# Final norm ahead of the overflow branch, a router norm for each half of the rows, and gated products on VectorE: a single-core diffusion block

## The chip, the cores and the metric

The kernel runs on one core of one Trainium2 chip. A core has the matmul engine TensorE (PE, its weight loads are listed apart as PEld), VectorE (DVE), ScalarE (ACT), GpSimd (POOL) and SyncE (SP), and DMA engines that move data between HBM and the on-chip memories. The metric is the device time of one execution in microseconds (us). The time before is the median of three runs; the trace is one more execution under the hardware profiler.

## What is computed

One layer of a diffusion backbone on 256 latent rows of 1024 features, with 256 rows of context. Cut to what matters here:

```
h      = modulate(rms_norm(x, g_mix))             # also for the context
u,v,yg,xr,ga,gb = split(h @ w_in + b_in)
a_lat  = layer_norm(conv31(u * sigmoid(v)));  a_lat = silu(a_lat) @ w_pa
y_rec  = rglru forward + rglru backward           # linear scans along the rows
b_lat  = (gelu(yg) * y_rec) @ w_pb                # the gated products
x      = x + gt1 * ((sigmoid(ga) * a_lat + sigmoid(gb) * b_lat) @ w_o)
hm     = modulate(rms_norm(x, g_ffn))             # the router's norm
gates  = top-1 of 4 groups, top-2 of 4 experts in it, from hm @ w_grp, hm @ w_er
x      = x + gt2 * sum over experts of swiglu(hm; w_gate, w_up, w_down) * gates
return   rms_norm(x, g_final)                     # the final norm
```

All is float32. A large matmul is made of float32r pieces: each operand is split into a high part (a ScalarE copy to float32r) and a low part (a subtraction), and three products are added.

## The kernel before

`hybrid_block` holds the whole layer. Rows lie in two blocks of 128 (index b), features in two halves of 512 (index h) or eight tiles of 128 (index t). Weights of `w_in`, `w_pb`, `w_pa` and `w_o` arrive as `raw` tiles; ScalarE (L291) and VectorE (L292) split each into `ws`, and `project` (matmuls on L307) uses them. Expert weights `ew` stream in through SyncE's and GpSimd's queues as their buffers come free. What stands on each engine comes from a scheduler, which may move instructions; those given to `pin` (`tc.keep_in_program_order`), `fix` and `in_order` keep their written order.

Four places matter.

**Gated products.** After the scans, the gate `gT` is multiplied by the scans' sum `yl` in four pieces of 128x512 (`prods`, L796), ScalarE rounds each to `mh` (L800), and the rest goes to `ml` (L801). Both L796 and L801 run on GpSimd. Behind that the layer norm of the convolution branch: squares `t` of `yc` (L816, ScalarE, out of the same pool `tmp` of rotating buffers as the products), their mean by a matmul (L817), `lm` (L819), a root, `yc` times the root (L824), swish, and the split into `ah` (ScalarE) and `al` (L831, GpSimd). `mh`, `ml` feed the `w_pb` projection and `ah`, `al` the `w_pa` projection; L844 merges the first into the sum.

**Root.** `rsqrt` takes a shift and a subtraction on the bits, and three Newton steps. For a width of 2 each step runs column by column (L207, L210), otherwise on the whole (L212 to L214).

**Router.** In the `w_o` loop each block gets its residual (L956, L957), the modulated `xs` (L959), the square sums `ssq2`, a transpose, and logits (`logits`, L935). `stay_warm(n)` issues n matmuls without use (L915) to keep TensorE busy; `WARM` has the four counts. After both blocks the root of both columns is taken at once (`ms2`, L986), the logits are scaled (`lg20`, L990), ranked, and the chosen experts' mask `mskb` (L1070) goes to the counting matmul `utri` (L1074). From the counts come positions and the one-hot rows `sg`, and only then the low parts `xsl` of the second half (`low_part`, L920), which gather matmuls (L1029) read.

**Tail.** Four groups of experts run with fixed capacities. Then a condition (`count(0)`, kept in `cint`) says whether any expert has overflowed; if so, nested blocks of extra work run. With these inputs they do not. Behind the branch (L1381) comes the final norm: `ms3` (L1394) and its root, two products with `gfin` on GpSimd (L1399) that ScalarE scales, two on VectorE (L1403), and the output's transfers, two from SyncE's queue (L1404) and two from ScalarE's (L1406).

## Time and profile before

| what | value |
|---|---|
| median of three runs | 604.14 us (604.13 to 605.14) |
| the profiled execution, its own time | 605.15 us |
| its span in the trace | 603.3 us |
| mean granted TensorE clock | 0.977 |
| busy: PE, PEld, DVE, ACT, POOL | 562.9, 371.7, 332.1, 249.1, 115.5 us |
| bytes moved | 182.86 MB, mean 303 GB/s |

The span is what the trace covers; the execution's own time is 1.85 us longer. Busy times are sums over each engine's instructions; engines run side by side, so they don't add up to the span. Idle time before an instruction is put down to what ended last before it started.

### The profile page before, as it was taken

The numbers are of one execution on the slowest core, as the hardware profiler recorded it, in microseconds if no ns is written. First come the engines' busy times: TensorE is split into PE (matmuls) and PEld (weight loads), VectorE is DVE, ScalarE is ACT, GpSimd is POOL, SyncE is SP. The second block draws the span as 40 slices with busy tenths as digits, with TensorE's granted clock in tenths as the row PEclk, the third lists the DMA queues.
The fourth block names the chain that finished last, engine by engine and source line by source line (L and its number), as shares of the span: only waits on it lengthen the run. The fifth ranks groups of instructions, "written<-read, shape, count | busy, mean of one in ns | idle before, by whom it ended". The sixth has DMA issues, their size and how long they took to land. (4 is left out here: it accounts for less than half of the span.)

```text
span 603.3 us, 9530 instructions
## 1 busy us (share of the span) xinstructions
PE 562.9 (93%) x3864; PEld 371.7 (62%) x3864; DVE 332.1 (55%) x658; ACT 249.1 (41%) x394; POOL 115.5 (19%) x122
## 2 busy tenths in 40 slices
PE   9989899999999999998999999969999999999980
PEld 8778777767667687788999787333335335333420
DVE  4724784821088978998897757623143404523224
ACT  4315524465954999646583552120012002101101
POOL 0000200001000100028072000333333431244301
PEclk9989899999999999999999999998999999999996
DMA  8982897368454467757975966799999999999942
GB/s 342 421 359 82 312 380 265 122 241 346 140 198 148 182 212 279 279 202 284 423 283 210 381 258 266 297 422 420 422 422 421 420 422 421 375 377 422 419 175 73
DMA packets 31326, 182.86 MB, mean 303 GB/s; under 512 B 3710, under 2 KB 8086, under 8 KB 10796
## 3 DMA queue, kind: packets, MB, share of 16 engines
q1 hardware_dynamic: 18812, 98.21, 42.9%
q0 software_dynamic: 12032, 83.35, 33.8%
q8 instruction: 32, 0.52, 0.4%
q10 hardware_dynamic: 432, 0.62, 0.3%
q14 instruction: 18, 0.15, 0.1%
HBM read 179.53 MB, written 2.64 MB: 302 GB/s over the span
## 5 line engine op out<-in xcount | busy, mean ns | idle before, releaser
L292 DVE TENSOR_TENSOR ws<-raw,ws 128x1024 fp32r<-128x1024 f32 x72 | 92.2, 1302 | 66.8 <-ACT ws L291 62.7
L307 PE MATMUL acca<-hxh,ws 128*128 128x256 f32 (+1 forms) x384 | 106.3, 320 | 2.4 <-ACT hxh L258 2.0
L307 PE MATMUL accb<-hxh,ws 128*128 128x256 f32 (+1 forms) x384 | 99.6, 302 | 0.0
L291 ACT ACTIVATE ws<-raw 128x1024 fp32r<-128x1024 f32 x72 | 74.2, 1053 | 26.4 <-PE accb L307 14.9
L307 PEld LDWEIGHTS acca<-hxh,ws 128*128 128x128 f32 x384 | 68.0, 192 | 16.9 <-issue 9.9
L307 PEld LDWEIGHTS accb<-hxh,ws 128*128 128x128 f32 x384 | 68.1, 192 | 2.9 <-ACT th L388 0.4
L1237 PE MATMUL acca<-ew,hg 128*64 128x512 f32 (+1 forms) x320 | 59.2, 595 | 0.0
L307 PE MATMUL acca<-hxl,ws 128*128 128x256 f32 (+1 forms) x192 | 55.2, 305 | 0.1
L307 PE MATMUL accb<-hxl,ws 128*128 128x256 f32 (+1 forms) x192 | 54.8, 303 | 0.0
L1237 PE MATMUL accb<-ew,hg 128*64 128x512 f32 (+1 forms) x256 | 45.1, 594 | 0.0
L307 PEld LDWEIGHTS acca<-hxl,ws 128*128 128x128 f32 x192 | 37.1, 193 | 4.4 <-issue 2.9
L597 POOL DMA_INDIRECT ew<-in_w_gate_dram,idxd x24 | 23.2, 967 | 86.8 <-PE acca L1237 45.9
L1237 PEld LDWEIGHTS acca<-ew,hg 128*64 128x64 f32 (+1 forms) x320 | 17.2, 126 | 35.5 <-issue 34.5
L307 PEld LDWEIGHTS accb<-hxl,ws 128*128 128x128 f32 x192 | 37.2, 194 | 1.3
L1250 PE MATMUL accb<-ew,at 128*32 128x512 f32 (+1 forms) x128 | 25.7, 675 | 6.2 <-DMA ew<-in_w_down_dram 3.9
L1200 ACT ACTIVATE yh<-yv 128x512 fp32r<-128x512 f32 x12 | 7.6, 630 | 56.5 <-DVE yv L1195 56.5
L667 PE MATMUL side<-xc,gw 128*128 128x512 f32 x64 | 30.6, 602 | 0.0
L1212 DVE TENSOR_TENSOR xt<-xt,side 128x512 f32<-128x512 f32 x28 | 18.2, 684 | 21.1 <-PE side L1211 21.0
L597 POOL DMA_INDIRECT ew<-in_w_down_dram,idxd x24 | 22.8, 951 | 36.3 <-issue 12.4
L1250 PE MATMUL acca<-ew,at 128*64 128x512 f32 (+1 forms) x128 | 25.4, 654 | 4.6 <-ACT at L1291 2.6
L1237 PEld LDWEIGHTS accb<-ew,hg 128*64 128x64 f32 (+1 forms) x256 | 12.8, 123 | 27.2 <-issue 27.2
L377 PE MATMUL side<-z,csw 128*32 128x256 f32 x512 | 29.0, 380 | 0.0
(343 smaller groups left out, 986.2 us busy)
## 6 DMA issues: line engine op xcount, KB each, us to landing
raw<-in_w_in_dram SPq DMA_DIRECT2D x24, 1024.0 KB
raw<-in_w_rows_dram SPq DMA_DIRECT2D x16, 1024.0 KB
wsc<-in_w_mod_dram SPq DMA_DIRECT2D x8, 1024.0 KB
ew<-in_w_gate_dram SPq DMA_DIRECT2D x8, 1024.0 KB
ew<-in_w_up_dram SPq DMA_DIRECT2D x8, 1024.0 KB
ew<-in_w_down_dram SPq DMA_DIRECT2D x8, 1024.0 KB
z<-zd POOLq DMA_DIRECT2D x8, 766.0 KB, 7.7
csw<-in_conv_s_dram SPq DMA_DIRECT2D x4, 1024.0 KB
```

What stands on the lines that cost most here:

```text
L291: S.activation(w[:, 0], src, AF.Copy)
L292: io(V.tensor_tensor(w[:, 1], src, w[:, 0].bitcast(F32), op=ALU.subtract))
L307: ins = io(T.matmul(o, l[pr[0]], r[pr[1]], start=start and first.get(i) == j and not (paired and i % 2), stop=stop and j >= len(n) - m and ...
L377: T.matmul(o[32 * i:32 * i + 32], csw[t // 2][:, t % 2, i, m], z[:, i, :, 4 * m:4 * m + 64], start=(m == 0), stop=(m == 7))
L597: return P.indirect_dma_start(out=t.rearrange("p k c -> p (k c)"), out_offset=None, in_=wex[key].rearrange("e (r k) c -> (e r) (k c)", k=m ...
L667: T.matmul(o1, gws[g][:, d, m, t], xcs[g][:, t].rearrange("p s n -> p (s n)"), start=True, stop=True)
L1200: S.activation(yh, yv, AF.Copy)
L1212: V.tensor_tensor(xt[:, b, cs], xt[:, b, cs], po, op=ALU.add)
L1237: fix(T.matmul(o[j][n * i:n * i + n, :], sl(i, k), wt[p, key, i, k // 4][:, k % 4, :], start=(k == 0), stop=(k == 7)))
L1250: fix(T.matmul(od[c][n * i:n * i + n, :], at[:, k, n * i:n * i + n], wt[p, 2, i, h][:, k % 2, 512 * c:512 * c + 512], start=(k == 0), stop ...
```

## The change

In words: (1) the products `prods` and the remainders `ml` of the gated products are issued on VectorE instead of GpSimd. (2) A new function `root(b)` takes the root of one block's `ssq2` alone, right after that block's logits in the second half of the `w_o` loop; `low_part(0, 1)` is pinned right behind `root(0)` and no longer behind the one-hot rows; the scaling into `lg20` is pinned; `rsqrt` runs column by column for a width of 1 too; the third entry of `WARM` goes from 13 to 11. (3) A new function `final_norm()` is called ahead of the branch, and again inside the overflow block at its end (where the rows are written a second time, behind the first writes). In it one 128x512 piece is multiplied by `gfin` on VectorE before the root and scaled by ScalarE, the other three are made by VectorE in one operation each, and all four transfers are issued by SyncE.

```diff
-WARM = (3, 3, 13, 3)
+WARM = (3, 3, 11, 3)
...
         for _ in range(3):
-            if n == 2:
+            if n <= 2:
                 for b in range(n):
...
     for t in range(0, 8, 2):
         prods.append(tmp([128, 2, 256]))
-        P.tensor_tensor(prods[-1], gT[:, t:t + 2], yl[:, t:t + 2], op=ALU.mult)
+        V.tensor_tensor(prods[-1], gT[:, t:t + 2], yl[:, t:t + 2], op=ALU.mult)
...
         S.activation(mh[:, t:t + 2], prods[t // 2], AF.Copy)
-        P.tensor_tensor(ml[:, t:t + 2], prods[t // 2], mh[:, t:t + 2].bitcast(F32), op=ALU.subtract)
+        V.tensor_tensor(ml[:, t:t + 2], prods[t // 2], mh[:, t:t + 2].bitcast(F32), op=ALU.subtract)
...
+    r2s = [None, None]
+
+    def root(b):
+        in_order[0] = V.engine
+        ms2 = cp.tile([128, 1], F32, name=f"ms2{b}")
+        io(V.scalar_tensor_tensor(ms2, ssq2[:, b, 0:1], EPS, ssq2[:, b, 1:2], op0=ALU.add, op1=ALU.add))
+        r2s[b] = rsqrt(ms2, [128, 1], lambda s, n: cp.tile(s, F32, name=f"r2{b}" + n))
+        in_order[0] = T.engine
...
                 logits(b, h, turn(b, h))
+                root(b)
+                if b == 0:
+                    pin(low_part(0, 1))
...
-    ms2 = cp.tile([128, 2], F32, name="ms2")
-    after(V.scalar_tensor_tensor(ms2, ssq2[:, :, 0], EPS, ssq2[:, :, 1], op0=ALU.add, op1=ALU.add), x_ins)
-    r2 = rsqrt(ms2, [128, 2], lambda s, n: cp.tile(s, F32, name="r2" + n))
-    r2s = [r2[:, b:b + 1] for b in range(2)]
     for b in range(2):
-        V.scalar_tensor_tensor(lg20[:, b], plg[b], r2s[b], br20, op0=ALU.mult, op1=ALU.add)
+        pin(V.scalar_tensor_tensor(lg20[:, b], plg[b], r2s[b], br20, op0=ALU.mult, op1=ALU.add))
...
     sg0 = slots_of((pos[:, :, STATIC[0]:STATIC[0] + 4], CAP // 2), first=True)
-    pin(low_part(0, 1))
     pin(low_part(1, 1))
...
+    def final_norm():
+
+        xg = [[tmp([128, 512], name="xg") for _ in range(2)] for _ in range(2)]
+        ms3 = eps[0].tile([128, 2], F32, name="ms3", tag="ms3", bufs=2)
+        V.tensor_tensor(xg[0][0], xt[:, 0, 0:512], gfin[:, 0:512], op=ALU.mult)
+        V.scalar_tensor_tensor(ms3, ssq3[:, :, 0], EPS, ssq3[:, :, 1], op0=ALU.add, op1=ALU.add)
+        r3 = rsqrt(ms3, [128, 2], lambda s, n: eps[0].tile(s, F32, name="r3" + n, tag="r3" + n, bufs=2))
+        S.activation(xg[0][0], xg[0][0], AF.Copy, scale=r3[:, 0:1])
+        for b, h in ((0, 0), (1, 0), (1, 1), (0, 1)):
+            hs = slice(512 * h, 512 * h + 512)
+            if b + h:
+                V.scalar_tensor_tensor(xg[b][h], xt[:, b, hs], r3[:, b:b + 1], gfin[:, hs], op0=ALU.mult, op1=ALU.mult)
+            ins = dma(ov_[:, b, hs], xg[b][h])
...
+    written = {}
+    final_norm()
+
+
     with tc.If(count(0) > 0):
         extra_pair()
...
-    for h in range(2):
-        hs = slice(512 * h, 512 * h + 512)
-        P.tensor_tensor(xg[h], xt[:, 0, hs], gfin[:, hs], op=ALU.mult)
-    r3 = rsqrt(ms3, [128, 2], lambda s, n: cp.tile(s, F32, name="r3" + n))
-    for h in range(2):
-        hs = slice(512 * h, 512 * h + 512)
-        V.scalar_tensor_tensor(xg[2 + h], xt[:, 1, hs], r3[:, 1:2], gfin[:, hs], op0=ALU.mult, op1=ALU.mult)
-        dma(ov_[:, 1, hs], xg[2 + h])
-        S.activation(xg[h], xg[h], AF.Copy, scale=r3[:, 0:1])
-        dma2(ov_[:, 0, hs], xg[h])
+        final_norm()
```

How it moves instructions: VectorE, around the gated products, where `t_...` are the products, L292 the weight splits, L710 to L714 the end of the scans; rows of the kernel before carry a minus, of the changed one a plus.

```order
+L796 TENSOR_TENSOR t_2715<-gT,yl 128x512
+L796 TENSOR_TENSOR t_2717<-gT,yl 128x512
 L712 SCALAR_TENSOR_TENSOR t_2567<-la,t_2567,lt 128x256
 L714 TENSOR_TENSOR yl<-yl,t_2567 128x256
-L292 TENSOR_TENSOR ws<-raw,ws 128x1024 x6
+L292 TENSOR_TENSOR ws<-raw,ws 128x1024 x2
+L801 TENSOR_TENSOR ml<-t_2715,mh 128x512
+L796 TENSOR_TENSOR t_2719<-gT,yl 128x512
+L796 TENSOR_TENSOR t_2721<-gT,yl 128x512
+L292 TENSOR_TENSOR ws<-raw,ws 128x1024
+L801 TENSOR_TENSOR ml<-t_2717,mh 128x512
+L292 TENSOR_TENSOR ws<-raw,ws 128x1024 x2
```

The eight operations of GpSimd now stand between the weight splits on VectorE; two more of `ml` and two splits follow, and then `lm`, with seven splits ahead of it in all where there were six.

Further on, on VectorE too, one split has left the root of the layer norm and the first pair of merges (L844) stands ahead of `yc`.

```order
-L292 TENSOR_TENSOR ws<-raw,ws 128x1024
 L212 TENSOR_TENSOR rst<-rsy 128x256
 L213 TENSOR_TENSOR rst<-rst,rsh 128x256
 L214 SCALAR_TENSOR_TENSOR rsy<-rst,rsy 128x256
-L824 TENSOR_TENSOR yc<-yc,rsy 128x256 x8
 L844 SCALAR_TENSOR_TENSOR tga_2345<-tga_2345,acca 128x512
 L844 SCALAR_TENSOR_TENSOR tga_2345<-tga_2345,accb 128x512
+L824 TENSOR_TENSOR yc<-yc,rsy 128x256 x8
```

One of the two splits inside the root is gone, and the merges, which stood behind `yc`, have moved in front of it.

VectorE in the router before, from the second half's first block on (`t_3601`: block 0, `t_3623`: block 1):

```order
L956 TENSOR_TENSOR t_3601<-acca,rw_3104 128x512
L957 TENSOR_TENSOR xt<-xt,t_3601 128x512
L959 TENSOR_TENSOR xs<-xt,rw_3104 128x512
L956 TENSOR_TENSOR t_3623<-accb,rw_3104 128x512
L957 TENSOR_TENSOR xt<-xt,t_3623 128x512
L959 TENSOR_TENSOR xs<-xt,rw_3104 128x512
L986 SCALAR_TENSOR_TENSOR ms_3666<-ssq_3425 128x2
L199 TENSOR_SCALAR r2rsy<-ms_3666 128x2
```

And the same place after the change, with line numbers of the changed kernel:

```order
L968 TENSOR_TENSOR xs<-xt,rw_3104 128x512
L954 SCALAR_TENSOR_TENSOR ms_3623<-ssq_3425 128x1
L199 TENSOR_SCALAR r20rsy<-ms_3623 128x1
L200 TENSOR_SCALAR r20rsy<-r20rsy 128x1
L201 TENSOR_SCALAR r20rsh<-ms_3623 128x1
L207 SCALAR_TENSOR_TENSOR r20rst<-r20rsy,r20rsh 128x1
L210 SCALAR_TENSOR_TENSOR r20rsy<-r20rst,r20rsy 128x1
L207 SCALAR_TENSOR_TENSOR r20rst<-r20rsy,r20rsh 128x1
L210 SCALAR_TENSOR_TENSOR r20rsy<-r20rst,r20rsy 128x1
L207 SCALAR_TENSOR_TENSOR r20rst<-r20rsy,r20rsh 128x1
L210 SCALAR_TENSOR_TENSOR r20rsy<-r20rst,r20rsy 128x1
L920 TENSOR_TENSOR xsl<-xs,xsh 128x8x64
```

The first block's root and its low part stand between the two blocks; the residual of block 1 (L965 now) follows them.

SyncE at the end of the changed kernel: the four output transfers (L1402) stand behind the last expert weights and ahead of the branch.

```order
L596 DMA ew<-in_w_down_dram 128x2048 x8
L1181 TENSOR_LOAD cint
L1181 ISA x2
L1402 DMA out_dram<-xg 128x512 x4
L1413 COMPARE_AND_BRANCH
```

The reading of the condition (L1181) comes before the transfers, the branch itself after them.

## Rows read from the trace of the kernel before

**Rows 1.** Busy times by stretch: us, then PE, PEld, DVE, ACT, POOL, clock, DMA share, GB/s.

```profile
280.00:290.00 10.00, 8.06 (x54) 7.17 (x54) 5.61 (x6) 5.67 (x10) 6.49 (x4) 1.00 1.01 418
384.00:420.00 36.00, 31.08 (x201) 12.85 (x194) 10.00 (x19) 5.44 (x12) 14.84 (x16) 0.91 1.01 422
598.40:601.30 2.90, 0.00 (x0) 0.00 (x0) 0.00 (x0) 0.00 (x0) 0.00 (x0) 0.50 0.97 362
```

**Rows 2.** Timeline of ScalarE and TensorE, 280 to 320: start, duration, ..., [idle before].

```profile
285.29 0.42 ACT L816 ACTIVATE t<-yc 128x256 f32<-128x256 f32 x1 [1.79 <-POOL ml L801]
...
285.76 0.70 PE L817 MATMUL misc<-t,inv 128*128 128x256 f32 x2 [1.51 <-ACT t L816]
...
318.78 0.39 PE L307 MATMUL acca<-al,ws 128*128 128x256 f32 x1 [1.10 <-POOL al L831]
```

**Rows 3.** Groups of instructions on POOL: count, busy us, mean ns, idle before.

```profile
L796 POOL TENSOR_TENSOR t<-gT,yl 128x512 f32<-128x512 f32 x4 | 8.3, 2075 | 47.9 <-DVE lt L697 33.9 <-DVE yl L714 13.9
L801 POOL TENSOR_TENSOR ml<-t,mh 128x512 fp32r<-128x512 f32 x4 | 7.9, 2002 | 0.0
```

**Rows 4.** Timeline of the tail, VectorE, ScalarE, POOL and SyncE.

```profile
588.71 0.69 DVE L1212 TENSOR_TENSOR xt<-xt,side 128x512 f32<-128x512 f32 x1 [0.17 <-PE side L1211]
...
589.97 0.19 ACT L1228 ACTIVATION_READ_ACCUMULATOR t<-xt 128x1 f32 x1
...
592.66 2.48 POOL L1399 TENSOR_TENSOR xg<-xt,gfin 128x512 f32<-128x512 f32 x2 [28.70 <-DVEq L1381]
...
592.69 1.25 DVE L1394 SCALAR_TENSOR_TENSOR ms<-ssq 128x2 f32<-128x2 f32 x1 [3.29 <-DVEq L1381]
...
596.98 1.42 DVE L1403 SCALAR_TENSOR_TENSOR xg<-xt,r3rsy,gfin 128x512 f32<-128x512 f32 x2
...
597.76 1.00 SPq L1404 DMA_DIRECT2D out_dram<-xg  x2
```

**Rows 5.** Timeline of TensorE at the last expert weights.

```profile
581.23 3.19 PE L1250 MATMUL acca<-ew,at 128*32 128x512 f32 x25 [1.41 <-DMA ew<-in_w_down_dram,idxd]
```

**Rows 6.** Timeline of VectorE in the router.

```profile
363.05 0.69 DVE L956 TENSOR_TENSOR t<-accb,rw 128x512 f32<-128x512 f32 x1 [3.28 <-PE accb L307]
...
365.32 0.16 DVE L986 SCALAR_TENSOR_TENSOR ms<-ssq 128x2 f32<-128x2 f32 x1
...
367.82 0.24 DVE L990 SCALAR_TENSOR_TENSOR lg<-side,r2rsy,br 128x20 f32<-128x20 f32 x1 [0.21 <-PE side L935]
...
370.07 0.19 DVE L1070 TENSOR_TENSOR mskb<-best,two 128x32 bf16<-128x32 f32 x1
...
371.68 2.12 DVE L920 TENSOR_TENSOR xsl<-xs,xsh 128x512 fp32r<-128x512 f32 x2
```

**Rows 7.** Timeline of VectorE around the gated products.

```profile
274.01 7.90 DVE L292 TENSOR_TENSOR ws<-raw,ws 128x1024 fp32r<-128x1024 f32 x4
...
288.15 1.23 DVE L292 TENSOR_TENSOR ws<-raw,ws 128x1024 fp32r<-128x1024 f32 x1 [4.01 <-PE accb L307]
```

**Rows 8.** Timeline of TensorE in the router.

```profile
367.62 3.25 PE L915 MATMUL accb<-xsh 128*128 128x512 f32 x13
370.72 0.18 PE L1074 MATMUL side<-mskb,utri 128*128 128x16 bf16 x1
...
373.85 0.66 PE L1029 MATMUL misc<-sg,xsl 128*128 128x128 f32 x4 [0.23 <-DVE xsl L920]
```

**Rows 9.** The branch's instructions: count, duration ns (least, median, most), first and last start.

```profile
L1381 DVEq EVENT_SEMAPHORE  x2: 21/21/21, 592.5 to 592.6; - x2
L1381 SPq COMPARE_BRANCH  x1: 50/50/50, 385.1 to 385.1; - x1
L1381 SPq EVENT_SEMAPHORE  x1: 17/17/17, 385.7 to 385.7; - x1
L1381 DVEq COMPARE_BRANCH  x1: 72/72/72, 589.5 to 589.5; - x1
```

**Rows 10.** SyncE's semaphores at the end: columns as in the group before.

```profile
L1455 SPq EVENT_SEMAPHORE  x8: 27/28/28, 601.7 to 602.2; - x8
```

More of the change, by code (lines that the diff above doesn't have):

```diff
@@ L1378, in hybrid_block @@
     fixed[0] = False
+    ov_ = out[0].rearrange("(b p) d -> p b d", p=128)
+    def final_norm():
[10 more added lines that the diff above has]
+            ins = dma(ov_[:, b, hs], xg[b][h])
+            if (b, h) in written:
+                tc.add_manual_dep(ins.ins, written[b, h].ins.name,
+                                  mybir.DependencyInfo(mybir.DependencyClass.Sync, mybir.DependencyReason.DATA),
+                                  reason="rows written again")
+            written[b, h] = ins
+    written = {}
+    final_norm()
     with tc.If(count(0) > 0):
@@ L1390, in hybrid_block @@
                         extra_pair()
-    ms3 = cp.tile([128, 2], F32, name="ms3")
-    V.scalar_tensor_tensor(ms3, ssq3[:, :, 0], EPS, ssq3[:, :, 1], op0=ALU.add, op1=ALU.add)
-    ov_ = out[0].rearrange("(b p) d -> p b d", p=128)
-    xg = [tmp([128, 512], name="xg") for _ in range(4)]
-    for h in range(2):
-        hs = slice(512 * h, 512 * h + 512)
-        P.tensor_tensor(xg[h], xt[:, 0, hs], gfin[:, hs], op=ALU.mult)
-    r3 = rsqrt(ms3, [128, 2], lambda s, n: cp.tile(s, F32, name="r3" + n))
-    for h in range(2):
-        hs = slice(512 * h, 512 * h + 512)
-        V.scalar_tensor_tensor(xg[2 + h], xt[:, 1, hs], r3[:, 1:2], gfin[:, hs], op0=ALU.mult, op1=ALU.mult)
-        dma(ov_[:, 1, hs], xg[2 + h])
-        S.activation(xg[h], xg[h], AF.Copy, scale=r3[:, 0:1])
-        dma2(ov_[:, 0, hs], xg[h])
+        final_norm()
 _INS = ["x", "ctx", "b_ada", "w_r_f", "w_i_f", "w_r_b", "w_i_b", "g_ffn",
```

## The prediction

> **What bounds the kernel now.** I read the busy times by stretch first, then the idle times of the engine that has none to spare, then the last 15 us. TensorE is busy for 93% of the span, so outside the tail only an idle time of TensorE can be won. Three places have some. Between 280 and 290 us it is busy 8.06 of 10.00 us [rows 1], and the largest single stall there is 1.51 us ahead of a variance matmul that waits for ScalarE's square [rows 2]. That square had itself waited 1.79 us for POOL's `ml`, whose reading frees the buffer that the square writes [rows 2]. So POOL, an engine with little to do, sets the pace: its four products take 2.08 us each and its four remainders 2.00 each [rows 3]. The second place is the router, 363 to 374 us, a chain of short operations that VectorE and TensorE hand to each other. The third is the tail: VectorE's last addition begins at 588.71 and the last square ends at 590.16 (589.97 + 0.19) [rows 4], yet the span ends at 603.3. Between router and tail the weights stream: from 384 to 420 us the DMA share is 1.01 at 422 GB/s [rows 1], and TensorE waits 1.41 us for the last of them at 581.23 [rows 5]. Time won ahead of that stream is kept only if the stream starts earlier by as much.
>
> **Part 1: the gated products on VectorE.** Added there: 8 operations of 128x512 on two inputs. An operation of that size took 0.69 us on VectorE [rows 6], so 8 x 0.69 = 5.5 us. Removed from POOL: 8.3 + 7.9 = 16.2 us [rows 3]. What VectorE gets back is its own speed while POOL ran: four weight splits took 7.90 us beside POOL, while one that ran alone took 1.23 [rows 7]; 7.90 - 4 x 1.23 = 3.0 us on that row, and the splits and scans on either side of it are also inside POOL's 16.2. So the added 5.5 us is offset by at least 3.0. VectorE moreover stood idle for 4.01 us at 284 to 288, waiting for TensorE [rows 7]. The net cost on VectorE up to there is hidden by that idle time, with 1.5 us to spare even against the row of 3.0.
>
> The page's rule and the row are not quite the same here. The Trainium skill (GPSIMD Engine Reference, section 4.1 Engine selection) puts two-input elementwise work at about twice VectorE's time on GpSimd; by that the eight would cost VectorE an estimated 8.1 us instead of 5.5, and part 1 would have 2.6 us less of cover. The trace has the operation on both engines and gives about three to one (2.00 to 0.69) while both are at work, so the sum goes by the row.
>
> What TensorE gets: the 1.51 us stall, since the squares no longer wait for POOL. Whether the chain behind it (`lm`, root, `yc`, ScalarE, `al`, the `w_pa` matmuls) keeps that is set by VectorE's order: one more split (1.23) stands ahead of `lm`, one fewer (1.23) inside the root, and two merges (2 x 0.69 = 1.38 by the 128x512 row that reads PSUM too [rows 6]) ahead of the eight `yc`. Net 1.38 later on VectorE, so in the worst case TensorE keeps 1.51 - 1.38 = 0.1. Against that, the chain starts on an engine with the 4.01 us of idle time in front of it. There is a second stall of 1.10 us at 318.78, for `al` on POOL [rows 2]. `al` stays on POOL, but VectorE's pieces ahead of its last two blocks stand earlier by one split (1.23 us); I count half of the stall, 0.5. Part 1: 1.5 + 0.5 = **2.0 us**, between 0.1 and 1.51 + 1.10 plus the rest of the 1.94 us of idle time in 280 to 290, which is 3.0.
>
> **Part 2: the router.** The root of one half took, with both halves interleaved, from 365.32 until 367.37: `lg` at 367.82 had been free to go 0.21 us earlier, at 367.61, which is the first `lg` (0.24) after the root, so the root is 2.05 us [rows 6]. Now there are two, of at most 2.05 each. The first one, and the split that is moved up (1.06 of 2.12 for two), are put where VectorE idled 3.28 us for TensorE ahead of 363.05 [rows 6]: 2.05 + 1.06 = 3.11, which just fits; without that cover it would be 3.1 us. The second root stands where the old one stood and ends before the logits, for which `lg` waited anyway: 0. What is won: the 13 warming matmuls ran 3.25 us, 0.25 each, and `utri` followed at 370.72, while its input `mskb` was there at 370.07 + 0.19 = 370.26 [rows 6, 8]. Two fewer are worth up to 0.50, limited to 0.46. Only one split is left behind the one-hot rows, so the 0.23 us that TensorE waited for the second goes [rows 8]. Part 2: 0.46 + 0.23 = **0.7 us**, between 0.4 (the 3.11 overruns the gap by a little) and 1.0 (weight loads that wait for the same split).
>
> **Part 3: the tail.** Before, the order was: last square, jump, root, products, transfers, end. The jump: VectorE reads the condition at 589.5 and goes on at 592.5, 3.0 us [rows 9]. SyncE paid 0.6 for its own (385.1 to 385.7) [rows 9]. Behind the jump VectorE and POOL got in each other's way: POOL's two products 2.48 us and `ms` beside them 1.25 [rows 4], where the like operation in the router took 0.16 [rows 6]. After: the one product that needs no root (0.69) runs from 589.40 beside the last square; `ms` at 590.2; root 2.05, to 592.25; three products at 1.42 / 2 = 0.71 [rows 4], to 594.4. ScalarE's piece runs beside the first of these. SyncE issues four transfers at 1.00 / 2 = 0.5 [rows 4], the last by 594.9. Before, the bytes ended at 601.3 [rows 1], 2.9 us behind VectorE's last product (596.98 + 1.42 = 598.40); after, 594.4 + 2.9 = 597.3 at the latest, and 596.4 if the earlier start of three transfers counts. From the bytes' end to the span's end it was 603.3 - 601.3 = 2.0 us, the semaphores of [rows 10] among it. That gives 598.4 to 599.3. VectorE's jump now begins 0.8 us after its last product starts (589.5 - 588.71, the same distance), at 594.5, and lands at 597.5, beside the transfer; with the 1.1 us from the semaphores at 602.2 to the end that is 598.6, not later. I take 599.2, near the late end, because all four transfers are on one queue now. Part 3: 603.3 - 599.2 = **4.1 us**, between 3.2 (the fourth rival) and 4.9.
>
> **The sum.** 2.0 + 0.7 + 4.1 = 6.8. The profiled execution took 605.15; 605.15 - 6.8 = 598.35. The runs' median is 604.14, 1.01 below the profiled one, so 598.35 - 1.01 = **597.3 us**.
>
> **The rivals.**
> - Normalisation chain late: the two merges ahead of `yc` hold the chain by 1.38, and the `al` stall stays. Part 1 is 0.1, the time 597.3 + 1.9 = 599.2. For it: the whole chain from `lm` to `yc` is VectorE's own work. Against: its 4.01 us of idle time.
> - The weight stream does not shift: it runs at 1.01 throughout, and if its start is tied to something other than the router's end, parts 1 and 2 are swallowed by the wait at 581.23. 604.14 - 4.1 = 600.0. Against: the stream's first stretch begins at 384, when buffers of earlier stages come free, which TensorE does.
> - The tail's jump is last: SyncE now reads its condition behind the last issue, not 200 us ahead. If its jump then takes 3.0 as VectorE's does, and not 0.6: 594.9 + 0.6 + 3.0 = 598.5, with semaphores 0.5 and 1.1 to the end 600.1, so part 3 is 3.2 and the time 598.2. The Trainium skill (Runtime: NRT & Kernel Launch, section Instruction fetch mechanics) says that a taken branch whose target lies outside the pages held forces a fetch before execution continues; the 3.0 us of VectorE agrees with it, the 0.6 of SyncE does not show one, and by the rule SyncE's jump is of the slow kind if its target has moved off.
> - VectorE is the bound (the slower side): POOL's removal gives VectorE nothing back, because the slow splits have another cause (ScalarE's writes to the same tiles). Then 5.5 + 1.4 = 6.9 us stand on VectorE between 262 and 300, on the chain to `yc`, and the kernel is slower as soon as this exceeds what parts 2 and 3 give, 4.8: 604.14 + 6.9 - 4.8 = 606.2. For it: the work on VectorE is certain and the relief is inferred. Against: 7.90 / 4 = 1.98 against 1.23 per split [rows 7], and the 4.01 us.
> - The change doesn't do what it says: the transfers, written ahead of the branch, are awaited by SyncE before it jumps, since the branch may write the same rows again. The jump then stands behind the bytes: 597.3 + 0.5 + 3.0 + 1.1 = 601.9, part 3 is 1.4, the time 600.0.
>
> **How the numbers follow.** Forecast 60% (own range 596.0 to 598.7, from part 1 at 3.0 with part 2 at 1.0 on one side to half of each on the other); chain late 14%; stream unmoved 11%; jump last 7%; transfers awaited 2%; VectorE the bound 3%; and 3% for a partial case of the last kind that ends near 604. The runs of this kernel tell about 0.2%, 1.2 us, from no change. Faster 94%, same 3%, slower 3%. The range 595.6 to 600.4 takes in the forecast, the late chain, the last jump and the unmoved stream.
>
> **What would show it.** Part 1: TensorE's idle time in the ten us from 280 on falls from 1.94 to about 0.4, no square waits for `ml`, and the splits on VectorE there take 1.2 us; wrong if `yc` starts no earlier relative to the stage's start. Part 2: `utri` follows two 0.25 us matmuls earlier, the root of the first half lies wholly in front of the second half's `t`. Part 3: no idle time between the last square and `ms`, `ms` at about 0.16 us, the last issue about 5 us behind the last square, and the end 9 us behind it, not 13. If the first weight stretch at full DMA share does not begin some 2.7 us earlier, the stream did not shift. The prediction is wrong if the splits stay slow without POOL.

## The result and the profile after

The changed kernel took **594.91 us** (median of six runs, 592.54 to 596.56) beside 604.05 us of the kernel before (median of six, 601.83 to 605.14): a ratio of **0.9853**, interval 0.9827 to 0.9879, which is 8.9 us less. The forecast was 597.3 in a range of 595.6 to 600.4. It had the sign and the mechanisms, and the time lies 0.7 us below the range.

The same pair was measured in three more sets of runs, each on a chip of its own; they matter for how the 594.91 is read:

```
                            this kernel     before        ratio (95% interval)
the changed kernel          594.91 (6 runs) 604.05 (6)    0.9853 (0.9827 to 0.9879)
the same again, e8          597.09 (6)      605.11 (23)   0.9865 (0.9836 to 0.9893)
the same again, e10         594.48 (5)      603.68 (11)   0.9843 (0.9816 to 0.9870)
the same again, f2          596.25 (6)      603.38 (11)   0.9879 (0.9849 to 0.9909)
```

The mean of the four ratios is 0.9860, 8.5 us. The profiled execution of the changed kernel is at 592.54 the quickest of its six, 2.4 us below their median, and that of before, at 605.15, is 1.0 us above the median of the three runs that the prediction had. So the 12.5 us between the two spans (603.3 and 590.8) are not what the change is worth, and the next rows have to be read by stage. One of the 12 executions of e4 below took 642.84 us at a mean granted clock of 0.84, and the ratio given there leaves it out.

The windows that answer to [rows 1], of the changed kernel (us, then busy time of PE, PEld, DVE, ACT, POOL, the clock, the DMA share and GB/s):

```profile
280.00:290.00 10.00, 10.00 (x81) 9.84 (x80) 7.42 (x15) 3.12 (x5) 0.00 (x0) 1.00 1.02 425
300.00:320.00 20.00, 19.81 (x166) 19.61 (x165) 17.62 (x24) 14.12 (x25) 10.42 (x8) 1.00 0.74 273
```

TensorE has no idle time left from 280 to 290 where it had 1.94 us, and 0.19 us from 300 to 320 where it had 1.48.

The squares and the variance matmuls that answer to [rows 2], ScalarE first, then TensorE:

```profile
272.23 1.02 ACT L816 ACTIVATE t<-yc 128x256 f32<-128x256 f32 x3
...
277.62 2.32 PE L817 MATMUL misc<-t,inv 128*128 128x256 f32 x10
```

No square waits for `ml` any more; ten of the sixteen variance matmuls run back to back.

The weight splits of the whole kernel on VectorE (the count, then between the bars busy us and the mean of one in ns), from the page of after:

```profile
L292 DVE TENSOR_TENSOR ws<-raw,ws 128x1024 fp32r<-128x1024 f32 x72 | 86.2, 1220 | 63.0 <-ACT ws L291 62.8
```

The 72 splits took 92.2 us before, 1302 ns each, and 86.2 now: VectorE gets 6.0 us back, more than the 5.5 us that it takes over.

The router, answering to [rows 6] and [rows 8], VectorE and then TensorE:

```profile
357.58 0.69 DVE L965 TENSOR_TENSOR t<-accb,rw 128x512 f32<-128x512 f32 x1 [0.20 <-PE accb L307]
...
359.84 0.16 DVE L954 SCALAR_TENSOR_TENSOR ms<-ssq 128x1 f32<-128x1 f32 x1
...
362.37 0.24 DVE L998 SCALAR_TENSOR_TENSOR lg<-side,r21rsy,br 128x20 f32<-128x20 f32 x1 [0.43 <-PE side L935]
...
362.18 2.77 PE L915 MATMUL accb<-xsh 128*128 128x512 f32 x11
364.87 0.17 PE L1082 MATMUL side<-mskb,utri 128*128 128x16 bf16 x1
```

The idle time of 3.28 us ahead of the second block is down to 0.20: the first root and the split that was moved up fill it and do not overrun. `lg` of block 1 still waits for TensorE (0.43 us), so the second root costs nothing.

The tail, answering to [rows 4] and [rows 9], VectorE, SyncE, and the branch's instructions (count, duration in ns, first and last start):

```profile
581.52 0.16 DVE L1395 SCALAR_TENSOR_TENSOR ms<-ssq 128x2 f32<-128x2 f32 x1 [0.19 <-ACT t L1235]
...
583.61 2.08 DVE L1401 SCALAR_TENSOR_TENSOR xg<-xt,r3rsy,gfin 128x512 f32<-128x512 f32 x3
...
584.24 2.47 SPq L1402 DMA_DIRECT2D out_dram<-xg  x4
...
L1413 DVEq EVENT_SEMAPHORE  x2: 21/21/21, 588.0 to 588.1; - x2
...
L1413 DVEq COMPARE_BRANCH  x1: 72/72/72, 584.4 to 584.4; - x1
L1413 SPq COMPARE_BRANCH  x1: 45/45/45, 587.1 to 587.1; - x1
```

`ms` follows the last square by 0.03 us (it ends at 581.49) and takes 0.16. The last issue ends at 584.24 + 2.47 = 586.71. VectorE's jump, 584.4 to 588.0, now runs beside the transfers.

**The stages.** Five marks cut each trace into stages that can be compared, whatever happened ahead of them. In us: from the start of the last gate matmul of the scans (L667) to the start of the last residual (`t<-accb`); from there to `utri`; to the first addition of experts' output to the rows; to the last such addition; from the last square's read to the end of the span. The last column says whether VectorE pauses for 2.4 us ahead of the first `hg` in the first expert group, of which more below.

```
                     products  router  group 1  groups   tail   pause
before                  106.7     7.7     45.5   172.5   13.3   no
e1  tail alone          106.8     7.7     46.0   172.8    9.5   no
e2  products alone      103.2     7.7     46.3   174.9   13.5   no
e3  router alone        106.8     7.3     45.8   173.1   13.3   no
e4  all but the tail    103.1     7.3     46.0   173.3   13.2   no
e5  before, five extra  106.8     7.7     44.9   175.5   13.3   no
e7  before, three extra 106.7     7.7     43.1   172.4   13.3   no
e8  after               103.1     7.3     46.2   175.2    9.5   no
after                   103.2     7.3     42.7   172.4    9.5   yes
e9  after, extra        103.2     7.3     48.5   173.5    9.5   yes
e10 after               103.2     7.3     42.8   173.0    9.4   yes
e11 ml alone            104.1     7.7     43.4   176.7   13.3   yes
e12 products only       103.8     7.7     43.4   173.8   13.5   yes
e13 after, 13 warming   103.2     7.7     43.6   174.3    9.4   yes
f1  before              106.8     7.7     43.2   174.3   13.2   yes
f2  after               103.2     7.3     43.1   172.3    9.7   yes
```

Three stages are steady to 0.3 us and show the change: 3.5 us for the products, 0.4 for the router, 3.8 for the tail, **7.7 us** together. The two expert stages move by 4 us and more from trace to trace, and e8 and f1 below show that the pause is not the change's. Ahead of all of them, the last gate matmul started at 254.2 to 256.8 us in the traces, 2.6 us apart; before had 256.3 and after 254.4.

### The profile page after: what moved, and what is told of

Read it like the earlier page. It is cut to its first block, busy times and chain, and to the rows that moved or that the text cites. A ratio compares the mean times of both kernels' runs of the same rounds, so it can differ in the third digit from the quotient of the medians.

```text
span 590.8 us, 9521 instructions
## 1 busy us (share of the span) xinstructions
PE 558.8 (95%) x3862; PEld 370.3 (63%) x3862; DVE 331.4 (56%) x672; ACT 248.3 (42%) x393; POOL 93.2 (16%) x112
## 5 line engine op out<-in xcount | busy, mean ns | idle before, releaser
L292 DVE TENSOR_TENSOR ws<-raw,ws 128x1024 fp32r<-128x1024 f32 x72 | 86.2, 1220 | 63.0 <-ACT ws L291 62.8
L1041 ACT ACTIVATE hg<-hg,sh 128x256 f32<-128x256 f32 (+1 forms) x32 | 13.3, 473 | 42.0 <-DVE hg L1039 41.8
L667 PE MATMUL side<-xc,gw 128*128 128x512 f32 x64 | 30.6, 602 | 0.0
```

Of the source, the lines that this page charges most:

```text
L292: io(V.tensor_tensor(w[:, 1], src, w[:, 0].bitcast(F32), op=ALU.subtract))
L667: T.matmul(o1, gws[g][:, d, m, t], xcs[g][:, t].rearrange("p s n -> p (s n)"), start=True, stop=True)
L1041: S.activation(dst[:, k], dst[:, k], AF.Identity, bias=sh8[:, k:k + 1])
```

## The experiments

**Each part alone.** e1 to e3 take the kernel before and put one part of the diff in. e1 has the new tail:

```diff
+    written = {}
+    final_norm()
     with tc.If(count(0) > 0):
...
-    for h in range(2):
-        hs = slice(512 * h, 512 * h + 512)
-        P.tensor_tensor(xg[h], xt[:, 0, hs], gfin[:, hs], op=ALU.mult)
...
+        final_norm()
```

> The kernel before with the final norm ahead of the branch and nothing else of the change. The parts add up (theory A): the way from the last square to the span's end was 13.1 us in the trace of before and is 9.3 in that of after, so this is 3.8 us faster, about 600.2 us beside 604.05. Rival (B), that the excess of the measured gain over the forecast came from the tail: 5 to 6 us faster. Stage by stage nothing ahead of the last square moves by more than the run-to-run spread.

Measured: 602.54 us (12 runs) beside 605.38 (30), 0.9951 (0.9934 to 0.9968): 3.0 us, between 1.9 and 4.0. The stage shows 3.8. Theory A holds, rival B falls.

e2 has the two lines of the gated products:

```diff
-        P.tensor_tensor(prods[-1], gT[:, t:t + 2], yl[:, t:t + 2], op=ALU.mult)
+        V.tensor_tensor(prods[-1], gT[:, t:t + 2], yl[:, t:t + 2], op=ALU.mult)
...
-        P.tensor_tensor(ml[:, t:t + 2], prods[t // 2], mh[:, t:t + 2].bitcast(F32), op=ALU.subtract)
+        V.tensor_tensor(ml[:, t:t + 2], prods[t // 2], mh[:, t:t + 2].bitcast(F32), op=ALU.subtract)
```

> The kernel before with the gated products and their remainders on VectorE and nothing else. Theory A (the stalls behind POOL cost TensorE 1.94 us in 280 to 290 and 1.48 in 300 to 320, nearly all of it is won): 3.3 to 3.7 us faster, and the wait for the last weights of the first expert group (3.92 us) with the slow clock behind it stays as it is. Rival (C): the first group's extra 2.3 us belongs to this part too, because what counts there is how early the group starts: about 6 us faster, with the 26 matmuls behind the wait at 3.6 us and not 5.95. My recorded step gave 2.0.

Measured: 601.97 us (7 runs), 0.9938 (0.9917 to 0.9960): 3.8 us, between 2.4 and 5.0. TensorE in the first expert group (start, duration, ..., idle before and what ended it):

```profile
403.55 5.78 PE L1250 MATMUL accb<-ew,at 128*32 128x512 f32 x26 [3.92 <-DMA ew<-in_w_down_dram]
```

The wait of 3.92 us and the slow matmuls behind it are as they were in before. Theory A holds at 3.5 us; the rival C falls, and so does my recorded 2.0.

e3 has the router's part (`root`, `low_part(0, 1)`, the pinned `lg20`, 11 warming matmuls):

```diff
+    def root(b):
...
                 logits(b, h, turn(b, h))
+                root(b)
+                if b == 0:
+                    pin(low_part(0, 1))
...
-WARM = (3, 3, 13, 3)
+WARM = (3, 3, 11, 3)
```

> The kernel before with the root for each half, the split that is moved up and 11 warming matmuls, and nothing else. Theory A: 0.7 to 0.8 us faster, hardly told from the spread. Rival (D): the first expert group's 2.3 us come from here, since this part shifts the instructions of VectorE just ahead of that group, and VectorE's 2.4 us pause there (seen only after the change) lets the clock come back before the last weights are in: about 3 us faster.

Measured: 605.08 us (12 runs), 0.9989 (0.9974 to 1.0005): 0.7 us, not told from nothing by itself. The stage to `utri` is 7.3 us instead of 7.7, the first expert group 45.8. Theory A holds, rival D falls: the pause is not in this trace.

e4 has the products and the router together, with the old tail.

> The changed kernel with the old tail: gated products on VectorE and the router's part together. The sum of the two parts measured alone is 0.9938 x 0.9989 = 0.9927, 4.4 us faster. If this gives 4.4, what the whole change has over the sum of its parts (0.9853 beside 0.9951 x 0.9938 x 0.9989 = 0.9878, 1.5 us) needs the tail's part or is spread; if it gives 6 to 7 us, these two together change the first expert group: then its trace shows the last 26 matmuls of that group's second projection at about 3.6 us and a pause of VectorE ahead of it, as in after, and each part alone showed them at 5.8 to 6.6.

Measured: 602.0 us (12 runs) beside 605.11 (23), 0.9934 (0.9913 to 0.9956): 4.0 us, near the 4.4 that the two gave alone. The first group shows nothing new:

```profile
402.61 6.47 PE L1257 MATMUL accb<-ew,at 128*32 128x512 f32 x26 [3.95 <-DMA ew<-in_w_down_dram]
```

So the parts add up within their intervals: 0.9951 x 0.9934 = 0.9885, 7.0 us, and the stages say 7.7. What the trace of after has beyond that, in the first group, is in none of the parts' traces.

**The first expert group.** In after, TensorE waits 0.25 us for the last weights of the group and runs the 26 matmuls behind that in 3.62 us, where the parts alone wait 3.9 and take 5.8 to 6.6. And VectorE pauses ahead of `hg`, which stops TensorE for 3.15 us, earlier on. The clock falls behind that stop too (0.54 and 0.61 of full in the two stretches of 2 us from 390 on), but it is back at 1.00 by 394, before the 26 matmuls. TensorE in after, at these two places:

```profile
389.94 0.63 PE L1037 MATMUL misc<-sg,xsh 128*128 128x256 f32 x2 [3.15 <-DVE hg L1039]
...
400.51 3.62 PE L1257 MATMUL accb<-ew,at 128*32 128x512 f32 x26 [0.25 <-DMA ew<-in_w_down_dram]
```

My first theory was the clock: TensorE's idle time comes earlier and so the clock is back in time. e5 and e7 test it on the kernel before, by matmuls that keep TensorE at work in the wait:

```diff
+    def keep_busy(m, at):
+        if m:
+            t = side_bank()
+            for _ in range(m):
+                fix(T.matmul(t, at[:, 0, 0:128], gt2[:, 0:512], start=True, stop=True))
...
                     for i in range(ne):
+                        if p == 0 and h == 1 and c == 0 and k == 2:
+                            keep_busy((0, 1, 2, 2)[i], at)
```

> The kernel before with five extra matmuls (128x512, results not read) in the first expert group's second projection, ahead of the pieces whose weights arrive last, so that TensorE does not stand idle for 3.92 us there. Clock theory: the granted clock, 0.50 to 0.74 from 405 to 412 us in the trace of before, stays at 1.00, the 26 matmuls behind the wait take 3.6 us instead of 5.95, and the kernel is 2.3 us faster, about 601.7, though it does more work. Rival: the slow matmuls there are held by the weights and not by the clock: no change, or up to 1 us slower by the extra work.

Measured: 604.54 us (12 runs) beside 605.38 (30), 0.9985 (0.9967 to 1.0004): 0.9 us, not told from nothing. The trace has the 26 matmuls at full speed:

```profile
404.80 1.99 PE L1248 MATMUL side<-gt,at 128*128 128x512 f32 x4
406.71 3.62 PE L1258 MATMUL accb<-ew,at 128*32 128x512 f32 x26
...
578.88 6.54 PE L1258 MATMUL acca<-ew,at 128*32 128x512 f32 x26 [1.41 <-DMA ew<-in_w_down_dram,idxd]
```

So the clock theory is right about the first group. But five extra matmuls took longer than the wait, 1.7 us of the 2.3 were given back there, and the last group lost what was left: its own 26 matmuls behind the last weights took 6.54 us. e7 has three of them:

```diff
-                            keep_busy((0, 1, 2, 2)[i], at)
+                            keep_busy((0, 0, 1, 2)[i], at)
```

> The kernel before with three extra matmuls in the first expert group instead of five: five took 5.0 us where the wait and the small gaps before it hold 5.0 at most, and the last piece started 37.8 us behind utri beside 36.1 in before, so they gave back 1.7 of the 2.3 us. Clock theory: with 3.0 us of them the last piece starts where it did (36.1 behind utri), the 26 matmuls take 3.6 us, the first addition to the rows comes 2.3 us earlier against utri. Whether the end moves with it is the other question: if the weight stream's end bounds the kernel, 0 to 0.9 us is left, as with five; if TensorE does, 2.3.

Measured: 603.92 us (12 runs) beside 605.11 (23), 0.9988 (0.9968 to 1.0009): 0.7 us, again not told from nothing, though the first group of the traced execution is 2.4 us shorter than in before (43.1 and 45.5):

```profile
406.10 3.62 PE L1258 MATMUL accb<-ew,at 128*32 128x512 f32 x26 [1.05 <-DMA ew<-in_w_down_dram]
```

In the traced execution, at 601.82 the quickest of its twelve, the last group lost nothing (172.4). The median does not follow it. That the others spent the time won in the first group on waiting for the last weights, as e5's did, would explain this; one trace does not show it.

e8 is the changed kernel once more.

> The changed kernel as it is, once more beside the others on the same chip and with a second trace. If the pause of VectorE in the first expert group (2.4 us ahead of the first hg) and the full clock behind it belong to the kernel, this trace shows them again and the last weights arrive about 207.7 us behind utri; if they were one execution's, the trace looks like the parts' (3.9 us of waiting, 26 matmuls at about 6 us, last weights at 210 to 212), and the median sits at about 0.988 of before rather than 0.985.

Measured: 597.09 us (6 runs), 0.9865 (0.9836 to 0.9893). The pause is gone, from the same code. VectorE (DVE), then TensorE in the first group and in the last, then the clock in the first group (us, busy times, the clock third from the end, the DMA share and GB/s):

```profile
387.06 0.69 DVE L1039 TENSOR_TENSOR hg<-misc,rb 128x512 f32<-128x512 f32 x1 [0.51 <-PE misc L1037]
...
402.52 6.27 PE L1257 MATMUL accb<-ew,at 128*32 128x512 f32 x26 [3.94 <-DMA ew<-in_w_down_dram]
...
575.76 1.04 PE L1257 MATMUL acca<-ew,at 128*32 128x512 f32 x2 [1.42 <-DMA ew<-in_w_down_dram,idxd]
578.20 5.32 PE L1257 MATMUL acca<-ew,at 128*32 128x512 f32 x26 [1.40 <-DMA ew<-in_w_down_dram,idxd]
...
398.00:400.00 2.00, 0.59 (x2) 0.00 (x0) 0.00 (x0) 0.00 (x0) 0.00 (x0) 1.00 1.03 430
400.00:402.00 2.00, 0.00 (x0) 0.00 (x0) 0.00 (x0) 0.00 (x0) 0.94 (x1) 0.77 1.00 418
402.00:404.00 2.00, 1.48 (x8) 0.40 (x12) 0.00 (x0) 0.00 (x0) 0.05 (x1) 0.50 1.03 430
404.00:406.00 2.00, 2.00 (x16) 0.45 (x12) 0.00 (x0) 0.00 (x0) 0.88 (x1) 0.50 0.98 410
406.00:408.00 2.00, 2.00 (x13) 0.48 (x6) 1.12 (x2) 0.63 (x1) 0.94 (x1) 0.53 1.03 430
408.00:410.00 2.00, 2.00 (x8) 0.48 (x8) 1.07 (x2) 0.38 (x1) 0.94 (x1) 1.00 1.00 418
```

TensorE stands still for 3.94 us, the granted clock falls to 0.50 (1.2 of 2.4 GHz) while it waits, and it is back at 1.00 only some five us after work resumed: 6.27 us for matmuls that take 3.62 at full clock. So the pause does not come with the changed code as such: after, e8 and e10 are one kernel, and e8 alone is without it.

e9 carries the extra matmuls into the changed kernel, three in the first group and two in the last, as a version that might beat both; e10 is its partner without them.

```diff
+    BUSY = {0: (0, 0, 1, 2), len(groups) - 1: (0, 0, 1, 1)}
...
+                        if h == 1 and c == 0 and k == 2 and ne == 4 and p in BUSY:
+                            keep_busy(BUSY[p][i], at)
```

> The changed kernel with extra matmuls (128x512, results not read) ahead of the pieces of weights that arrive last: three in the first expert group, two in the last. Clock theory: in the first group utri to the first addition falls from 46.2 us (as in e8) to about 43.3, as in e7; in the last group the 26 matmuls behind the wait take 3.6 us and not 5.3 to 6.5, so that first to last addition is 172.4 and not 175. Against e8's median of 0.9865 of before this gives 1.5 to 3 us, a ratio of 0.982 to 0.984. Rival (the weight stream's end bounds everything): the first group's gain is spent in waiting for the last weights, and only the last group's part is left, 0 to 1.5 us: 0.984 to 0.9865.

> The changed kernel as it is, on the same chip as e9, as its partner and as a third measurement: 0.985 to 0.987 of before. By stages, if they are as steady as the traces so far: end of the gate matmuls to the last residual about 103.2 us, residual to utri 7.3, last square to the span's end 9.5; utri to the first addition 46 without the pause of VectorE, 42.7 with it.

Measured: e9 599.69 us (6 runs), 0.9925 (0.9897 to 0.9954); e10 594.48 (5), 0.9843 (0.9816 to 0.9870). With the extra matmuls the kernel is 5.2 us slower. Both traces have the pause. e9:

```profile
392.48 0.80 PE L1037 MATMUL misc<-sg,xsh 128*128 128x256 f32 x2 [3.27 <-DVE hg L1039]
...
398.97 5.95 PE L1267 MATMUL accb<-ew,at 128*32 128x512 f32 x36 [0.69 <-ACT at L1308]
404.85 1.12 PE L1257 MATMUL side<-gt,at 128*128 128x512 f32 x2
405.91 1.04 PE L1267 MATMUL accb<-ew,at 128*32 128x512 f32 x2
406.88 1.98 PE L1257 MATMUL side<-gt,at 128*128 128x512 f32 x4
408.80 3.62 PE L1267 MATMUL accb<-ew,at 128*32 128x512 f32 x26
```

and e10 at the same places:

```profile
391.38 0.80 PE L1037 MATMUL misc<-sg,xsh 128*128 128x256 f32 x2 [3.29 <-DVE hg L1039]
...
397.20 4.49 PE L1257 MATMUL accb<-ew,at 128*32 128x512 f32 x38 [0.76 <-ACT at L1298]
401.95 3.62 PE L1257 MATMUL accb<-ew,at 128*32 128x512 f32 x26 [0.25 <-DMA ew<-in_w_down_dram]
```

With the pause the wait for the last weights is already used up (0.25 us in e10), so the extra matmuls come on top: the three of the first group take 1.12 + 1.98 = 3.1 us. They are not the whole cost. The first group is 5.7 us longer in e9 than in e10, and part of that lies ahead of them: 36 matmuls took 5.95 us in e9 where 38 took 4.49 in e10, while the clock behind the pause stayed low until 402 in e9 and was back before 396 in e10 (the clock is the third number from the end; e9, then e10):

```profile
400.00:402.00 2.00, 2.00 (x16) 0.42 (x12) 0.00 (x0) 0.00 (x0) 0.00 (x0) 0.51 1.03 430
```

```profile
396.00:398.00 2.00, 1.24 (x12) 0.49 (x14) 0.58 (x5) 1.15 (x3) 0.74 (x1) 1.00 0.99 410
```

Why it stayed low longer in e9 is not shown. e7's cure is a cost here, and it is no version to keep. Both sides of the expectation were wrong: neither knew that the wait comes and goes from set to set.

**Chip or change?** Two runs settle where the pause belongs: f1 is the kernel before and f2 the changed one, on one chip, each with a trace.

> The kernel before, once more, for a trace on the same chip as f2. Nothing is left out. If the pause of VectorE in the first expert group (2.4 us ahead of the first hg) belongs to the chip and not to the change, the traces of f1 and f2 both show it or both don't, and utri to the first addition differs by less than 1 us between them. Rival: the pause belongs to kernels with the gated products on VectorE, in whole or in half (after, e9 to e13 show it, but e2, e4 and e8 don't): f1 shows none, with 45.5 us, and f2 may.

> The changed kernel beside f1 on one chip. If the chip makes the difference in the first expert group, what is left between the two traces is the steady part: gate matmuls' end to last residual 3.5 us, residual to utri 0.4, last square to end 3.8, together 7.7; and the measured ratio on this chip is 0.986 to 0.988. If the change itself wins 2.3 us in the first group, the sum is 10 and the ratio 0.983 to 0.984.

Measured: f1 602.58 us (one run), f2 596.25 (6 runs) beside 603.38 (11), 0.9879 (0.9849 to 0.9909). VectorE in f1 and then, in a fence of its own, in f2:

```profile
393.55 0.69 DVE L1031 TENSOR_TENSOR hg<-misc,rb 128x512 f32<-128x512 f32 x1 [2.40 <-remote]
```

```profile
391.41 0.69 DVE L1039 TENSOR_TENSOR hg<-misc,rb 128x512 f32<-128x512 f32 x1 [2.43 <-remote]
```

The kernel before has the pause too on this chip, 2.40 us beside 2.43, and its first group is as short (43.2 us) as that of the changed kernel (43.1). It is the chip, or the place of the program on it, or something else that the runs of one set share, and not the change. What remains between the two traces is the steady part: 3.6, 0.4 and 3.5 us. What makes VectorE pause is not shown: the trace names a releaser outside the core's engines and no more.

**The halves of the products' part, and the warming matmuls.** One trace each, without a timed comparison. e11 moves only the second of e2's two lines (`ml`), e12 only the first (`prods`).

> The kernel before with only the four remainders ml on VectorE, the products stay on POOL. Read from the trace: end of the gate matmuls to the last residual was 106.7 us in before and 103.2 with both moved. If the squares' wait for ml is what costs (my step), this alone takes 1.5 to 2.0 of the 3.5 us, and the stall ahead of the variance matmul is gone. If VectorE's slowness beside POOL is the larger cost, the products' last 4.45 us on POOL keep it, and 1 us or less is won.

> The kernel before with only the four products on VectorE, the remainders ml stay on POOL. Same stage as e11 (106.7 us in before, 103.2 with both moved). My step: the squares still wait for ml, whose four take 7.9 us on POOL, but they start some 4 us earlier, so that part of the 1.51 us stall goes and VectorE stays slow beside them: 0.5 to 1.5 us won. If e11 and e12 together give 3.5, the two moves are separate; if less, each needs the other.

The page's row for the weight splits, of e11 and then of e12 (between the bars: busy us and the mean of one in ns):

```profile
L292 DVE TENSOR_TENSOR ws<-raw,ws 128x1024 fp32r<-128x1024 f32 x72 | 89.5, 1262 | 62.3 <-ACT ws L291 62.2
```

```profile
L292 DVE TENSOR_TENSOR ws<-raw,ws 128x1024 fp32r<-128x1024 f32 x72 | 89.3, 1266 | 62.8 <-ACT ws L291 62.6
```

The one execution of each took 602.75 us (e11) and 601.75 (e12), which settles nothing. By the traces: with only `ml` moved the stage takes 104.1 us, 2.6 less than before; with only the products moved 103.8, 2.9 less; with both 3.5. So they are not separate, and either one takes most of it: with either alone, TensorE no longer waits for a square. What is left to 3.5 is the wait for `al`, which was 1.10 us in before [rows 2]. TensorE at that wait in e11, e12 and after:

```profile
314.47 0.39 PE L307 MATMUL acca<-al,ws 128*128 128x256 f32 x1 [1.10 <-POOL al L831]
```

```profile
315.76 0.39 PE L307 MATMUL acca<-al,ws 128*128 128x256 f32 x1 [0.69 <-POOL al L831]
```

```profile
313.05 0.38 PE L307 MATMUL acca<-al,ws 128*128 128x256 f32 x1 [0.19 <-POOL al L831]
```

The splits go the same way in both: 1302 ns before, 1262 and 1266 with half of the work gone from POOL, 1220 with all. I had expected less of both, least of e12.

e13 is the changed kernel with one number put back:

```diff
-WARM = (3, 3, 11, 3)
+WARM = (3, 3, 13, 3)
```

> The changed kernel with 13 warming matmuls in the third place again. Read from the trace: last residual to utri was 7.7 us in before and 7.3 after the change. My step gave the two matmuls 0.46 of that and the rest of the router part 0.23 behind utri: then this shows 7.7 to 7.8 us. If the early root is what shortens the way to the mask, it stays at 7.3.

```profile
363.66 3.23 PE L915 MATMUL accb<-xsh 128*128 128x512 f32 x13
366.73 0.18 PE L1082 MATMUL side<-mskb,utri 128*128 128x16 bf16 x1
```

Measured: 597.25 us, one run. The way from the last residual (359.06) to `utri` is 7.67 us again, as in before (363.05 to 370.72), beside 7.29 with 11 (357.58 to 364.87). So the two matmuls are all of what this stage won, 0.38 us and not my 0.46, and the early root shortens the way to the mask by nothing that shows.

## Why the prediction was right and wrong

**Part 1 is the step that failed, in its size: 2.0 us forecast, 3.5 measured.** The 1.51 us stall went as the prediction said, and its mechanism (POOL holds the squares, and slows VectorE's splits) is what the rows show. But the sum took nothing for the rest of the 1.94 us of idle time from 280 to 290 (0.43), and half of the wait for `al`, 0.5 of 1.10. The whole idle time went instead: 1.94 us in the ten us from 280 on and all but 0.19 of 1.48 in 300 to 320, together 3.2 us, and the stage is 3.5 us shorter in every trace with both moves; the 0.3 us between the two is not traced. The upper bound of 3.0 was too low too, since the 0.37 us that TensorE waited for a split near 303 stood in none of its terms.

Why the wait for `al` shrank is shown only in part. That its chain starts earlier is not enough: in e11 `yc` starts 37.7 us behind the last gate matmul (292.3 and 254.6), earlier than in before (40.3) and in after (39.1), and TensorE, which comes earlier too, still waits 1.10 us. VectorE's `yc` in before, then in e11:

```profile
296.63 2.77 DVE L824 TENSOR_TENSOR yc<-yc,rsy 128x256 f32<-128x256 f32 x8
```

```profile
292.35 2.77 DVE L824 TENSOR_TENSOR yc<-yc,rsy 128x256 f32<-128x256 f32 x8
```

The wait fell to 0.69 in e12 and 0.19 in after, and in these two the order on VectorE is the new one, with merges ahead of `yc` and two, not four, of the swish's multiplications in one go behind it; the longest `al` takes 3.5 us there and 4.6 in before and e11. Which part of the order does this, no run separates. The merges ahead of `yc`, which the prediction feared for up to 1.38 us, cost nothing that the stage shows.

**The price of the eight operations.** The prediction priced them at 0.69 us each. After the change a pair of products and a pair of remainders took 1.27 and 1.29 us on VectorE:

```profile
268.99 1.27 DVE L796 TENSOR_TENSOR t<-gT,yl 128x512 f32<-128x512 f32 x2
...
279.38 1.29 DVE L801 TENSOR_TENSOR ml<-t,mh 128x512 fp32r<-128x512 f32 x2
```

That is 0.64 each, a third of POOL's 2.0, which POOL needed beside VectorE. The trace of before also has one of them without VectorE beside it: the last `ml` starts at 285.2, inside VectorE's idle 4.01 us [rows 7], and takes the least of the four, 1.26 us (ns, least, median, most):

```profile
L801 POOL TENSOR_TENSOR ml<-t,mh x4: 1262/2244/2258, 278.6 to 285.2; 128x512 fp32r<-128x512 f32 x4
```

The Trainium skill (GPSIMD Engine Reference, section 4.1 Engine selection) puts two-input elementwise work on GpSimd at about twice VectorE's time. The trace agrees for POOL alone, 1.26 beside 0.64, and gives three to one and more while both work. For the sum the row was the better price.

**Part 2** was forecast at 0.7, and the stage to `utri` gives 0.4, all from the two warming matmuls (0.38 by e13, forecast 0.46). The cover held: 0.20 us of the gap is left. The 0.23 us behind `utri` went as well, and the experts' first matmul starts 5.0 us behind `utri` and not 5.5. Whether that half is kept is not shown: the first group takes 45.8 us in e3 and 45.5 in before, and without the pause and extra matmuls the traces lie between 45.5 and 46.3.

**Part 3** was forecast at 4.1 of 3.2 to 4.9 and came to 3.8 by the stage. Each of its marks was met: `ms` at 0.16, the last issue 5.2 us behind the last square (forecast 5), the end 9.3 (forecast 9). SyncE's jump took 0.2 us (587.1 to 587.3 for the instruction behind it), so the rival of the last jump fell. By the Trainium skill (Runtime: NRT & Kernel Launch, section Instruction fetch mechanics) a taken branch stalls if its target lies outside the pages held. The trace shows no such stall for SyncE at 0.2 us, and one of 3.6 us again for VectorE would agree with it; where the targets lay, no run shows. The transfers were not awaited ahead of the branch.

**The weight stream** shifted with the router, as the sum assumed: POOL's first expert load in the trace of after starts at 377.34 and not 383.66, 6.3 us earlier, of which 1.9 lie ahead of the change. What I did not see is that the groups behind it are not a fixed length. In ten of the sixteen traces the last 26 matmuls of the last group took 3.62 us, in six (e2, e5, e8, e11, e13, f1) 5.1 to 6.5, and in those six TensorE had waited longer for weights in that projection than in any of the ten: 1.42 + 1.40 = 2.82 us in e8, for one, beside 0.63 + 1.41 = 2.04 in before. In e8 the clock falls to 0.51 there. Since the longest wait of the ten, 2.73 us in e4, is close to the 2.82, it is not shown that the length of the wait alone decides.

**The sum.** 6.8 was forecast, the stages say 7.7, the four measured ratios 7.3 to 9.5 us with a mean of 8.5. The forecast counted from 604.14, the three runs that it had. The other three of the six beside the changed kernel took 601.83 to 603.96, with a median of 602.37, and elsewhere the kernel before measured 603.4 to 605.4. Of the 2.4 us by which 594.91 lies below 597.3, 0.9 is the sum of the parts (1.5 too little in part 1, 0.6 too much in the others). The remaining 1.5 us is no larger than the differences between sets of runs: the same kernel gave 597.09 and 596.25 in other sets, both inside the range, and 594.48 in a third, which is not. From 602.37 to 594.91 it is 7.5 us, close to the stages' 7.7, so a start of the sum that was too high for this set of runs may be part of it. It is not shown to be one cause; the trace of after has the pause that goes with a shorter first group, the trace of before that the prediction had does not.

**The slower rivals.** VectorE did not become the bound: it is busy 331.4 us in after and was 332.1, with eight operations more and the final norm's besides.

## What to carry to other kernels

Two engines that work side by side may slow each other: price a move from one to the other by what both lose while both run, and add up the idle time of the whole stage that hangs on it, not the one stall that names it. A chain that starts earlier does not by itself end a later wait for it, since the engine that waits comes earlier too. Work that stands behind a branch for no reason but order in the source belongs ahead of it, where the jump runs beside its transfers. Compare traces by stages with marks in the code, and take the two kernels on one chip before a difference in a stage that the change does not touch is given to the change.

## What the runs showed of the hardware

- A taken branch costs VectorE 3.0 to 3.6 us and SyncE 0.2 to 0.6, in the same program (589.5 to 592.5 and 385.1 to 385.7 before, 584.4 to 588.0 and 587.1 to 587.3 after).
- One weight split of 128x1024 on VectorE took 1.22 us, and 1.98 while POOL ran two-input operations. One of these, 128x512, took 1.26 us on POOL while VectorE stood idle and some 2.25 beside VectorE's work.
- Eight traces of four sets of runs have VectorE paused for 2.4 us at one place in the first expert group, whatever the kernel, while the weights streamed; the other eight, of three other sets, have no such pause. Its cause stays open.
- Filling a wait of TensorE with matmuls keeps its clock (26 matmuls at 3.62 us and not 5.95), but gave nothing that the medians of e5 and e7 tell from zero. In e9, where the wait was not there, three of them took 3.1 us of the first group, and the kernel was 5.2 us slower than e10.
